# A one-core float32 decoder block: more Strassen steps, x laid out by channel, the inverse root applied after the products

## The chip, the cores and the metric

The kernel runs on one core of a Trainium2 chip. The metric is the device time of one execution in microseconds (us), the median over runs. The profile of one execution is read beside it. The engines are PE (TensorE; its weight loads are listed as PEld and overlap the products), DVE (VectorE), ACT (ScalarE), POOL (GpSimd) and SP (SyncE, which here only issues DMAs). Each engine takes its own instructions strictly in order; they wait for each other by semaphores.

## The reference

For 256 tokens of 4096 channels, all in float32:

```python
h = rmsnorm(x, norm_w)                                   # x * 1/root(mean x^2 + eps) * norm_w
proj = einsum('bsd,de->bse', h, w_in)                    # 4096 -> 20480
u_p, z_p, u_c, b_c, c_c, z_c, g_logit = split(proj)      # 6 parts of 2048, one of 8192
y_pool = causal_multiscale_pool(u_p, pool_w, pool_scale) * silu(z_p)
y_conv = causal_gated_shortconv(u_c, b_c, c_c, conv_w, conv_b) * silu(z_c)
br = einsum('bsnc,ncd->bsnd', stack(y_pool, y_conv), w_branch)   # 2 x (2048 -> 4096)
merged = sum(sigmoid(g_logit + gate_b) * br)
x = x + einsum('bsd,de->bse', merged, w_out)             # 4096 -> 4096
return rmsnorm(x, final_norm_w)
```

The pooling takes a trailing mean of 2, 4, 8 or 16 tokens less the token itself, and then a 512x512 map for each of four groups. The short convolution is B * conv3(C * u).

## The kernel before

**Units and steps.** The output of every large product is cut into units of 1024 columns: 20 for w_in (named cu, cc, cb, cz for the convolution, pz, pu for the pool, g for the gates), 8 for w_branch (b0_c, b1_c), 4 for w_out (o0 to o3). A unit runs over its inner dimension in steps of 256 rows: 16 steps, or 8 in a branch unit. Each step loads one block of weights of 256x1024 (1 MB) on SP's queue into one of three buffers of `raw` (`NRAW = 3`, loads in turn, so a block takes the place of the one three steps earlier as soon as that one is prepared).

**High and low parts.** PE multiplies in fp32r, a rounded form. So every float32 operand is split: ACT writes the rounded high part, `act(h, q)` (line 62), and DVE the remainder, `sub(l, q, h)` (line 65). Each product is three matmuls: high by high, high by low, low by high. The parts of the weights lie in `ring`, a ring of 60 pieces of 256 columns; the parts of x (later of y and of the merged rows) stay in `arena`.

**P and S steps.** A P step is the plain product: two k blocks, two token blocks, two column halves, 24 matmuls of 128x512. Its preparation is one rounding on ACT and one subtraction on DVE, each 128x2048, and takes 16 pieces of the ring. An S step is one level of Strassen (Winograd's form): seven products, 21 matmuls. Its preparation is more work on DVE: the three blocks that are used as they are get one 128x1536 subtraction, four sums of weight blocks are made (one add of 128x1024 and two of 128x512), and the sums are rounded on ACT and subtracted on DVE two at a time (128x1024 each). It takes 12 + 8 + 8 pieces. Where two products of x operands are needed in sums, these are made once per operand (`sums_s`).

**Where the products go.** PSUM has four banks `sums` for results that need no recombination (called E) and four banks `shared` for the S products that are used in several places (called F). At the end of a unit ACT evacuates E with the inverse root of the norm as a scale, and `combine` (line 388) takes F apart: one copy on ACT, four operations of 128x512 and one of 128x2048 on DVE. `shared` also serves for transposes (line 416), the pooling (580 to 583, 601) and the start. After `combine` the unit's epilogue (`epi`) is put into a queue, of which one item is issued after every six matmuls (`TICK = 6`): gates, sigmoid, taps of the convolution, transposes, stores.

**Order.** All instructions are issued in the order in which the Python code makes them. `pump` (1003) lets preparation run up to three steps ahead of the matmuls (`AHEAD = 3`), as far as `raw` and `ring` have room. `Ring.alloc` (174) hands out and frees blocks in order. In a w_in unit of before the sequence is PPPPP SPSPSPSPSPS: 10 P and 6 S; the first unit has no S, but six N steps (plain products over both sets of banks). Branch units are PPPPPSPS. Altogether 154 S steps in 448.

**Start.** x arrives by tokens on SP's queue, and 64 transposes on PE (900) turn it; the S operands of x are prepared during the first unit, after the root is known (`x_stage`, `x_sums`, `x_fill`); PE also spreads the root over partitions (888).

Of the kernel before, what the change touches and what calls it, by code (L numbers as in the profile page):

```python
# [25 lines left out]
NP_X, NS_X = 10, 6  # L43
NP_Y, NS_Y = 6, 2
RING = 60
NRAW = 3
AHEAD = 3
# [3 lines left out]


@with_exitstack
def hybrid_block(ctx: ExitStack, tc: tile.TileContext, x, norm_w, w_in, pool_w, pool_scale,
                 conv_w, conv_b, gate_b, w_branch, w_out, final_norm_w, out):
    nc = tc.nc
    xf, of = x[0], out[0]
    win, wbr, wout, pw = w_in[0], w_branch[0], w_out[0], pool_w[0]
# [23 lines left out]
    def move(dst, src):  # L82

        return pin(nc.gpsimd.dma_start(dst, src))

# [9 lines left out]
    arena = sb("arena", [P, (4 * NP_X + 7 * NS_X) * KB], F32R)  # L95
# [5 lines left out]
    V = sb("V", [P, 2, NH])  # L101
    sa = sb("sa", [P, 8, P])
    ident = sb("ident", [P, P])
    par_n = sb("par_n", [P, 32])
    par = sb("par", [P, 64])
    rin = sb("rin", [P, 2])
    rout = sb("rout", [P, 2])
    ssq = sb("ssq", [P, 2, 8])
    ossq = sb("ossq", [P, 2, 5])


    PE0 = psum.tile([P, 2, NH], F32, name="sums0")
    PE1 = [psum.tile([P, NH], F32, name=f"sums1{n}") for n in range(2)]
# [3 lines left out]

# [5 lines left out]

    xhome = (R, E, Y, R)

    def xs(a, b, t=None):
        q = xhome[a // NU]
        s = slice(a % NU, (b - 1) % NU + 1)  # L130
        return q[:, :, s] if t is None else q[:, t, s]

    def load_x(a, b, queue=None):
        pin((queue or nc.sync).dma_start(xs(a, b), xrows[:, :, a:b]))
# [7 lines left out]


    def p_slot(i):

        return arena[:, 4 * KB * i:4 * KB * (i + 1)].rearrange("p (a k t c) -> p a k t c", a=2, k=2, t=2)

    def s_slot(i):

        o = 4 * KB * NP_X + 7 * KB * i  # L150
        return arena[:, o:o + 7 * KB].rearrange("p (a o c) -> p a o c", a=2, o=7)

    def sp_slot(i):

        o = 4 * KB * NP_X + 7 * KB * i
        return arena[:, o:o + 4 * KB].rearrange("p (a k t c) -> p a k t c", a=2, k=2, t=2)

    Q3, Q5, Q6, Q7, A12, A22, A11, A21 = range(8)

    class Operand:  # L160


        def __init__(self, kind, view, region):
            self.kind, self.view, self.region = kind, view, region
            self.ready = False

    busy = {}


    class Ring:  # L170
# [3 lines left out]
        def alloc(self, n):  # L174
            at = self.head if self.head + n <= self.size else 0
            for a, m, _ in self.live:
                if at < a + m and a < at + n:
                    return None
            if at == 0 and self.head + n > self.size and any(a >= self.head for a, _, _ in self.live):
                return None  # L180
            block = [at, n, False]
            self.live.append(block)
            self.head = at + n
            return block

        def release(self, block):
            block[2] = True
            while self.live and self.live[0][2]:
                self.live.pop(0)
# [3 lines left out]
    def piece(block, off, n):  # L193
        o = (block[0] + off) * KB
        return ring[:, o:o + n * KB]


    class Step:
        def __init__(self, unit, kind, src=None, op=None, **kw):
            self.unit, self.kind, self.src, self.op = unit, kind, src, op  # L200
            self.__dict__.update(kw)
            self.raw = None
            self.pre = []

        def micros(self):

            r = None if self.src is None else self.raw

            def both(block):
                self.h = piece(block, 0, 8).rearrange("p (k n) -> p k n", k=2)  # L210
                self.l = piece(block, 8, 8).rearrange("p (k n) -> p k n", k=2)
                self.block = block
                q = r.rearrange("p (k n) -> p k n", k=2)
                if self is steps[0]:
                    for k in range(2):
                        act(self.h[:, k], q[:, k])
                        sub(self.l[:, k], q[:, k], self.h[:, k].bitcast(F32))
                else:
                    act(self.h, q)
                    sub(self.l, q, self.h.bitcast(F32))  # L220

            if self.kind in "PN":
                return self.pre + [(16, None, both)]
            if self.kind == "S":
                q = r.rearrange("p (i n) -> p i n", i=4)
                tv = V

                def sums(_):
                    add(tv, q[:, 0:1].to_broadcast([P, 2, NH]), q[:, 1:3])

                def direct(block):
                    self.bd = block
                    self.dh = piece(block, 0, 6).rearrange("p (i n) -> p i n", i=3)
                    self.dl = piece(block, 6, 6).rearrange("p (i n) -> p i n", i=3)
                    act(self.dh, q[:, 1:4])
                    add(q[:, 0], tv[:, 0], q[:, 2])
                    sub(self.dl, q[:, 1:4], self.dh.bitcast(F32))
                    add(q[:, 1], q[:, 0], q[:, 3])

                def t13(block):  # L240
                    self.b13 = block
                    self.h13 = piece(block, 0, 4).rearrange("p (i n) -> p i n", i=2)
                    self.l13 = piece(block, 4, 4).rearrange("p (i n) -> p i n", i=2)
                    act(self.h13, tv)
                    sub(self.l13, tv, self.h13.bitcast(F32))

                def t24(block):
                    self.b24 = block
                    self.h24 = piece(block, 0, 4).rearrange("p (i n) -> p i n", i=2)
                    self.l24 = piece(block, 4, 4).rearrange("p (i n) -> p i n", i=2)  # L250
                    act(self.h24, q[:, 0:2])
                    sub(self.l24, q[:, 0:2], self.h24.bitcast(F32))

                return self.pre + [(0, None, sums), (12, None, direct), (8, None, t13), (8, None, t24)]
            if self.kind == "B":
# [7 lines left out]
                return [(16, lambda: self.unit.flags.get("base"), parts)]  # L263
            if self.kind == "M":
                g = self.g
                e = E.rearrange("p a n -> p (a n)")[:, g * 1024:(g + 1) * 1024].rearrange(
                    "p (k t) -> p k t", k=4)

                def weights(block):
                    self.bw = block  # L270
                    self.h = piece(block, 0, 8).rearrange("p (k n) -> p k n", k=4)
                    self.l = piece(block, 8, 8).rearrange("p (k n) -> p k n", k=4)
                    q = r.rearrange("p (k n) -> p k n", k=4)
                    act(self.h, q)
                    sub(self.l, q, self.h.bitcast(F32))

                def pooled(block):
                    self.ba = block
                    self.ah = piece(block, 0, 4).rearrange("p (k t) -> p k t", k=4)
                    self.al = piece(block, 4, 4).rearrange("p (k t) -> p k t", k=4)  # L280
                    act(self.ah, e)
                    sub(self.al, e, self.ah.bitcast(F32))

                return [(16, None, weights), (8, lambda: self.unit.flags.get(f"pooled{g}"), pooled)]

        def groups(self):

            gs = []
            if self is steps[0]:

                for k in range(2):
                    for i in range(3):
                        for t in range(2):
                            for n in range(2):
                                cs = slice(n * NH, (n + 1) * NH)
                                ah, al = self.op.standing(k, t)
                                h, l = self.h[:, k, cs], self.l[:, k, cs]
                                gs.append([("E", t, n), [((ah, h), (al, h), (ah, l))[i]], None])
                gs[-1][2] = [self.block]
            elif self.kind in "PN":  # L300
                for t in self.toks:
                    for n in self.halves:
                        cs = slice(n * NH, (n + 1) * NH)
                        mm = {"E": [], "F": []}
                        for k in range(2):
                            ah, al = self.op.standing(k, t)
                            h, l = self.h[:, k, cs], self.l[:, k, cs]
                            mm["F" if self.kind == "N" and k == 0 else "E"] += [(ah, h), (ah, l), (al, h)]
                        gs += [[(b, t, n), mm[b], None] for b in "FE" if mm[b]]
# [881 lines left out]
    while queue:  # L1191
        f = queue.popleft()
        if f:
            f()
# [61 lines left out]
```

## Time and profile before

| | |
|---|---|
| median of three runs | 2446.13 us (2446.05 to 2447.01) |
| span of the profiled execution, first to last instruction | 2444.0 us |
| granted clock, mean over the span | 0.997 |
| HBM read, written | 508.61 MB, 23.07 MB |
| wait of ACT `ring` for PE `sums` | 333.9 us in 137 waits |
| wait of DVE `ring` for ACT `ring` | 260.3 us in 251 waits |
| wait of PE `sums` for DVE `ring` | 11.7 us in 12 waits |

The profiled execution's time is its span; what the runs have above it, 2.1 us at the median, lies before the first and after the last instruction. In the rows of groups the columns are line, engine, operation, output<-input with shapes, count; then busy us and mean ns of one; then the idle time of the engine just before, with what ended most of it. In the rows of stretches each engine has its busy us and in brackets its instructions.

### The profile page before, as it was taken

The page shows a single profiled execution, that of the slowest core. Times are in us where ns is not written, and L with a number is a line of the kernel's source. Part 1 is how long each engine was busy: PE and PEld are TensorE (multiplying, and loading weights), DVE is VectorE, ACT ScalarE, POOL GpSimd, SP SyncE. Part 2 cuts the span into 40 slices and gives each one's busy share as a digit, 9 for nine tenths or more (in the row PEclk, how much of TensorE's full clock was granted, in tenths as well). Part 3 has the DMA queues.
Part 4 walks back from the last instruction along what each step waited for, and adds up shares of the span by engine and source line. Part 5 has one row for each costly group of instructions (what it writes and reads, how often), then busy time and mean ns, then how long its engine had stood idle before and what let it go on. Part 6 is the DMA issues. An engine that isn't in the chain of part 4 may idle for free.

```text
span 2444.0 us, 27058 instructions
## 1 busy us (share of the span) xinstructions
PE 2406.5 (98%) x10722; PEld 1987.0 (81%) x10722; DVE 2041.9 (84%) x1713; ACT 1296.7 (53%) x1089; POOL 61.6 (3%) x129
## 2 busy tenths in 40 slices
PE   9999999999999999999999999999999999999997
PEld 7888788888788888888888888887788888878886
DVE  5889789789888878968888888888888778888897
ACT  6545455555455545455555545555564455555554
POOL 0100000000000000000000000000000000000000
PEclk9999999999999999999999999999999999999999
DMA  7455565555566555556666666566667666666666
GB/s 276 172 207 204 180 219 207 206 207 189 189 214 216 193 194 212 193 189 224 236 224 219 220 229 232 195 240 229 239 231 252 219 233 238 227 229 225 232 229 260
DMA packets 137536, 533.45 MB, mean 218 GB/s; under 512 B 8832, under 2 KB 9408, under 8 KB 134592
## 3 DMA queue, kind: packets, MB, share of 16 engines
q1 hardware_dynamic: 126640, 483.42, 55.6%
q0 software_dynamic: 10432, 47.22, 5.2%
q8 instruction: 84, 1.38, 0.2%
q10 hardware_dynamic: 336, 1.07, 0.1%
q14 instruction: 44, 0.36, 0.0%
HBM read 508.61 MB, written 23.07 MB: 218 GB/s over the span
## 4 chain that ended last, share of the span: by engine, by line
PE 85%; DVE 6%; ACT 3%; issue 3%; DMA 2%; SPq 0%; POOL 0%; DVEq 0%; ACTq 0%; POOLq 0%
PE sums L1052 68%; PE shared L1052 15%; DVE ring L65 2%; ACT ring L62 2%; DVE R L65 2%; DMA raw<-in_w_out_dram 1%; PE shared L416 1%; PE shared L601 1%; DVE V L65 1%; DMA Y<-in_x_dram 1%; DVE raw L65 1%; ACT E L62 0%; DMA raw<-in_w_branch_dram 0%; PE shared L900 0%; ACT arena L62 0%
## 5 line engine op out<-in xcount | busy, mean ns | idle before, releaser
L1052 PE MATMUL sums<-ring,arena 128*128 128x512 f32 x8370 | 1968.0, 390 | 14.9 <-DVE ring L65 11.7
L1052 PEld LDWEIGHTS sums<-ring,arena 128*128 128x128 f32 x8370 | 1569.0, 188 | 345.2 <-DVE ring L65 16.4
L65 DVE TENSOR_TENSOR ring<-raw,ring 128x2048 fp32r<-128x2048 f32 (+2 forms) x607 | 1139.9, 1881 | 322.2 <-ACT ring L62 251.5
L62 ACT ACTIVATE ring<-raw 128x2048 fp32r<-128x2048 f32 (+2 forms) x607 | 946.8, 1585 | 756.6 <-PE sums L1052 306.1
L1052 PE MATMUL shared<-ring,arena 128*128 128x512 f32 x1884 | 475.1, 389 | 1.7 <-DVE ring L65 1.7
L1052 PEld LDWEIGHTS shared<-ring,arena 128*128 128x128 f32 x1884 | 353.4, 188 | 76.4 <-DVE ring L65 2.7
L62 ACT ACTIVATE ring<-V 128x1024 fp32r<-128x1024 f32 (+1 forms) x157 | 163.8, 1043 | 187.6 <-DVE V L65 164.1
L65 DVE TENSOR_TENSOR ring<-V,ring 128x1024 fp32r<-128x1024 f32 (+1 forms) x157 | 188.6, 1202 | 2.4 <-PE sums L1052 1.5
L65 DVE TENSOR_TENSOR V<-raw 128x1024 f32<-128x1024 f32 x154 | 187.8, 1219 | 0.9 <-DMA raw<-in_w_in_dram 0.9
L65 DVE TENSOR_TENSOR raw<-raw 128x512 f32<-128x512 f32 x154 | 106.6, 692 | 5.3
L65 DVE TENSOR_TENSOR raw<-V,raw 128x512 f32<-128x512 f32 x154 | 106.5, 692 | 4.8
L65 DVE TENSOR_TENSOR R<-R,E 128x2048 f32<-128x2048 f32 x41 | 93.9, 2291 | 8.6 <-DMA E<-in_x_dram 3.4
L65 DVE TENSOR_TENSOR R<-R,shared 128x512 f32<-128x512 f32 x90 | 61.7, 685 | 2.1
L62 ACT ACTIVATE E<-sums,rin 128x512 f32<-128x512 f32 (+1 forms) x60 | 45.3, 822 | 1.7 <-PE sums L1052 1.7
L62 ACT ACTIVATE arena<-sa 128x512 fp32r<-128x512 f32 (+1 forms) x24 | 17.3, 721 | 53.0 <-DVE sa L65 44.6
L65 DVE TENSOR_TENSOR R<-R,Y 128x2048 f32<-128x2048 f32 x17 | 38.9, 2289 | 0.3
L62 ACT ACTIVATE R<-R 128x2048 f32<-128x2048 f32 x8 | 15.4, 1919 | 42.6 <-DVE R L65 42.6
L416 PE MATMUL shared<-ident,R 128*128 128x128 f32 x192 | 28.3, 278 | 5.7 <-DVE R L65 5.7
L416 PEld LDWEIGHTS shared<-ident,R 128*128 128x128 f32 x192 | 23.7, 143 | 11.8 <-issue 4.5
L65 DVE TENSOR_TENSOR arena<-sa,arena 128x512 fp32r<-128x512 f32 (+1 forms) x24 | 19.3, 805 | 8.2 <-ACT arena L62 8.2
L601 PE MATMUL shared<-ring 128*128 128x512 f32 x96 | 22.1, 389 | 0.0
L62 ACT ACTIVATE E<-R 128x1024 f32<-128x1024 f32 (+1 forms) x10 | 13.9, 1396 | 15.1 <-DVE R L65 15.1
(151 smaller groups left out, 429.3 us busy)
## 6 DMA issues: line engine op xcount, KB each, us to landing
raw<-in_w_in_dram SPq DMA_DIRECT2D x319, 1024.0 KB, 4.8
raw<-in_w_branch_dram SPq DMA_DIRECT2D x64, 1024.0 KB, 5.6
raw<-in_w_out_dram SPq DMA_DIRECT2D x64, 1024.0 KB, 5.3
gates_d<-R POOLq DMA_DIRECT2D x8, 1024.0 KB, 8.9
raw<-in_pool_w_dram SPq DMA_DIRECT2D x4, 1024.0 KB, 5.2
Y<-in_gate_b_dram POOLq DMA_DIRECT2D x8, 512.0 KB, 11.3
Y<-gates_d POOLq DMA_DIRECT2D x4, 1024.0 KB, 10.3
E<-gates_d POOLq DMA_DIRECT2D x4, 1024.0 KB, 5.2
```

The source lines that it names most:

```text
L62: return pin(nc.scalar.activation(dst, src, func, **kw))
L65: return pin(nc.vector.tensor_tensor(out=dst, in0=a, in1=b, op=op))
L416: pin(nc.tensor.transpose(shared(j)[:, i * T + t * P:i * T + (t + 1) * P], src[:, t, c:c + P], ident))
L601: pin(nc.tensor.matmul(o, a[:, k, ts], b[:, k], start=(k, i) == (0, 0), stop=(k, i) == (3, 2)))
L1052: pin(nc.tensor.matmul(ps, lhs, rhs, start=n == 0, stop=n == u.total[b] - 1))
```

## The change

The lines below are from the kernel after; "..." marks what is left out.

Units have a text that gives their kinds of steps, and there are 195 S steps:

```diff
-NP_X, NS_X = 10, 6
-NP_Y, NS_Y = 6, 2
+ND, NS, NB = 8, 6, 2
-AHEAD = 3
+AHEAD = 4
+SIX5 = "PPPPPSPSPSPSPSPS"
+SIX4 = "PPPPSPSPSPSPSPSP"
+SEVEN3 = "PPPSPSPSPSPSPSPS"
+EIGHT = "PSPSPSPSPSPSPSPS"
+HOST = "PPPBPPMMPPSPSSPSSPS"
+OUT3 = "PSPSPSPSPSPSSPPP"
+B0 = "PPPPPSPS"
+B1 = "PSPPSPSP"
```

(B and M are the pooling steps.) In order: cz0 SIX5, cb0 EIGHT, cu0 SEVEN3, cc0 EIGHT, cz1 SIX4, cb1 EIGHT, cu1 SEVEN3, cc1 EIGHT, pz0 SIX4, pu0 EIGHT, pz1 HOST, pu1 EIGHT, g0_0 HOST, six gate units EIGHT, g1_3 SIX4, the branches B0 and B1 in turn, o0 SIX5, o1 and o2 EIGHT, o3 OUT3.

A step's preparation is cut in two, and ACT's first rounding of step i+1 is issued before the rest of step i. The ring keeps its 60 pieces; blocks are freed part by part:

```diff
+    def first(self):          # P: act(h, q) 128x2048;  S: act(dh, q[:, 0:3])
+    def rest(self):
+        if self.kind == "P":
+            def lows(_):
+                for ks in self.ks:
+                    sub(self.l[:, :, ks], self.q[:, :, ks], self.h[:, :, ks].bitcast(F32))
+        if self.kind == "S":
+            def direct(_):
+                sub(self.dl, self.q[:, 0:3], self.dh.bitcast(F32))
+            def t13(block):
...
+                add(q[:, 1::2], q[:, 3:4].to_broadcast([P, 2, NH]), q[:, 1:3])
+                act(self.h13, q[:, 1::2])
+                add(q[:, 2], q[:, 1], q[:, 2])
+            def t24(block):
...
+                add(q[:, 0], q[:, 2], q[:, 0])
+                act(self.h24, q[:, 0::2])
+                sub(self.l13, q[:, 1::2], self.h13.bitcast(F32))
+                sub(self.l24, q[:, 0::2], self.h24.bitcast(F32))
...
+    lay(0, steps[0].pre + steps[0].first())
+    for i in range(len(steps)):
+        if i + 1 < len(steps):
+            lay(i + 1, steps[i + 1].first())
+        lay(i, steps[i].rest() + [(None, None, lambda _, i=i: done(i))])
+        if i + 1 < len(steps):
+            lay(i + 1, steps[i + 1].pre)
```

The products of an S step run in the order M2, N3, M1, N7, N5, N4, N6 (the last of a unit: M2, N3, N4, M1, N7, N5, N6); M2, N3 and M1 use the direct part, N7 and N5 the pair `t13`, N4 and N6 the pair `t24`.

The operands of x carry norm_w but no root, which comes in at the joins:

```diff
+    def evacuate(u, t, n):
+        dst = E if u.s else u.dst
+        kw = dict(scale=rin[:, t:t + 1]) if u.scaled else {}
+        act(dst[:, t, n * NH:(n + 1) * NH], PE_[t][n], **kw)
+    def corners(d):
...
+        act(q(0, 1), shared(0))
+        add(q(1, 0), q(0, 1), shared(3))
+        add(q(1, 1), q(1, 0), shared(2))
+        sub(d[:, :, 0:NH], shared(1).rearrange("p (o n) -> p o n", o=1).to_broadcast([P, 2, NH]),
+            d[:, 1].rearrange("p (n c) -> p n c", n=2))
+    def combine(u):
...
+            if u.scaled:
+                for t in range(2):
+                    stt(d[:, t], d[:, t], rin[:, t:t + 1], E[:, t], ALU.mult, ALU.add)
+            else:
+                add(d, d, E)
```

x comes a second time, turned on the host (`xc`), 256 KB for each step of the first unit on SP's queue; the rows by tokens come on POOL's queue and serve only for the squares. The first unit has S steps; 64 + 2 transposes and the spreading of the root go:

```diff
+    def x_operand(j):
+        i = first_order[j]
+        o, q = x_ops[i], xt[:, j % 4]
+        if o.kind == "P":
...
+        else:
+            for k in range(2):
+                act(sa[:, 6 - 2 * k:8 - 2 * k], q[:, 2 - 2 * k:4 - 2 * k], scale=norm_col(2 * i + k))
+            sums_s(sa)
+            parts_of(o, sa[:, 0:o.n])
+    before(2, fetch_rows, 0)
+    before(2, fetch_rows, 1)
+    before(6, square, 0)
...
+    before(13, square, 3)
+    before(13, lambda: rstd_of(ssq, rin, "rin"))
```

Weights are laid out on the host so that a step's block is 8 KB in a row for each partition. silu is one activation of 128x2048 on ACT in place of a sigmoid and a multiplication; the convolution's units run in the order z, B, u, C, and its gates are multiplied by tokens, so that 32 transposes fall away; pool_scale is a column scale of an ACT copy:

```diff
+    def silu_y():
+        return gap(1) + [lambda: act(Y, Y, AF.Silu)]
+        def b_epi(u):
...
+            return gap(1) + [lambda: mul(R, R, Y)] + gap(4) + transposes(R, copy) + [lambda: move(g_d[c], Y)]
+        def c_epi(u):
+            items = gap(1) + [lambda: mul(R, R, Y)] + gap(3) + [lambda: move(E, g_d[c])]
...
+            return items + gap(4) + [lambda: mul(Y, Y, E), lambda: put(y_d[1, c], chan(Y))]
```

Epilogues of the gate, branch and out units are as before.

More of the change, by code (lines that the diff above doesn't have):

```diff
@@ L780, in hybrid_block @@
         branch_unit(1, c)
-    last_y = units[-2], units[-1]
     for c in range(4):
@@ L961, in hybrid_block @@
[L961 to L982 removed]
+        q = rows_tile(c)
@@ L987, in hybrid_block, with lay, done @@
         s.load_index = i
-    state = dict(limit=0, nl=0, np=0, micros=None, prepared=0, now=0, mm=0)
+    state = dict(limit=1, nl=0, mm=0, now=0)
+    work = deque()
+    def lay(i, items):
+        work.extend((i, size, guard, fn) for size, guard, fn in items)
+    def done(i):
+        steps[i].prepared = True
+    lay(0, steps[0].pre + steps[0].first())
[5 more added lines that the diff above has]
+            lay(i + 1, steps[i + 1].pre)
     queue = deque()
@@ L1035, in pump, with flush @@
                 return
-    for s in steps:
-        s.prepared = False
+    def flush():
+        while queue:
+            f = queue.popleft()
+            if f:
+                f()
     def tick():
@@ L1053, in multiply @@
             u.seen[b] = n + 1
-        for block in release or ():
-            rg.release(block)
+        for part in release:
+            rg.release(part)
         state["mm"] += len(mm)
     def after_group(u, b):
-        if b[0] == "E" and u is not last:
-            t = b[1]
-            if u.closed(("E", t, 0), ("E", t, 1)) and not u.flags.get(f"e{t}"):
-                u.flags[f"e{t}"] = True
-                evacuate(u, t)
+        if u is not last:
+            if b in u.total and u.closed([b]) and b not in u.flags:
+                u.flags[b] = True
+                if b[0] == "E":
+                    evacuate(u, b[1], b[2])
+                elif u.closed(FB):
+                    flush()
+                    corners(u.dst)
         while state["mm"] >= TICK:
```

856 lines of the change are left out of this document (318 added, 538 removed).

## The prediction

> **What bounds the kernel now.** I read the page first, then busy time by stretches, the chain of waits, groups by form, and the timeline of one join between two gate units.
>
> ```profile
> span 2444.0 us, 27058 instructions
> PE 2406.5 (98%) x10722; PEld 1987.0 (81%) x10722; DVE 2041.9 (84%) x1713; ACT 1296.7 (53%) x1089; POOL 61.6 (3%) x129
> ```
>
> ```profile
> 0.00:15.00 15.00, 10.50 (x33) 7.45 (x34) 5.87 (x8) 7.07 (x9) 2.01 (x9) 1.00 0.85 314
> 15.00:50.00 35.00, 34.10 (x174) 28.27 (x173) 26.57 (x45) 26.69 (x49) 0.76 (x1) 1.00 0.76 288
> 1394.00:1477.00 83.00, 83.00 (x368) 68.73 (x367) 68.30 (x52) 43.64 (x33) 1.06 (x2) 1.00 0.62 220
> 1700.00:1780.00 80.00, 72.81 (x312) 57.71 (x311) 70.28 (x68) 44.71 (x39) 5.90 (x11) 1.00 0.68 236
> 2432.00:2444.00 12.00, 0.00 (x0) 0.00 (x0) 5.19 (x13) 2.80 (x6) 0.00 (x0) 0.61 0.80 320
> ```
>
> PE sets the time. A gate unit (1394 to 1477) has PE busy throughout and DVE for 68.3 of 83.0; PE idles at the start, 7.2 us at the first branch units, and 12 us behind its last matmul.
>
> ```profile
> 1403.71 27.20 PE sums L1052 x120
> ```
>
> A large matmul costs 27.20/120 = 0.2267 us: a P step 5.44, an S step 4.76, a pair 10.20.
>
> **What goes from PE.**
>
> ```profile
> L1052 PE MATMUL sums<-ring,arena 128*128 128x512 f32 x8370 | 1968.0, 390 | 14.9 <-DVE ring L65 11.7 <-ACT ring L62 2.4 <-ACT E L62 0.8
> L1052 PE MATMUL shared<-ring,arena 128*128 128x512 f32 x1884 | 475.1, 389 | 1.7 <-DVE ring L65 1.7
> L900 PE MATMUL shared<-ident,R 128*128 128x128 f32 x32 | 5.5, 313 | 1.4 <-DMA R<-in_x_dram 1.4
> L416 PE MATMUL shared<-ident,R 128*128 128x128 f32 x192 | 28.3, 278 | 5.7 <-DVE R L65 5.7
> ```
>
> With 36 + 96 more, large matmuls were 448 x 24 - 154 x 3 + 96 = 10386. Now 195 x 3 are saved: 10263, 123 fewer, 27.9 us. Of transposes go 64 (line 900; this row has half) and 32 (line 416), at 28.3/192 = 0.15 us by busy time, overlaps in; I take 0.1, together 9.6, and 0.9 for six small ones. PE has 38.4 us less.
>
> **What DVE gets.** Timeline of DVE, then groups:
>
> ```profile
> 1407.15 1.40 DVE L65 TENSOR_TENSOR R<-R,shared 128x512 f32<-128x512 f32 x2
> 1409.91 2.29 DVE L65 TENSOR_TENSOR R<-R,E 128x2048 f32<-128x2048 f32 x1
> 1412.24 2.29 DVE L65 TENSOR_TENSOR R<-R,Y 128x2048 f32<-128x2048 f32 x1
> 1414.44 2.28 DVE L65 TENSOR_TENSOR ring<-raw,ring 128x2048 fp32r<-128x2048 f32 x1
> 1420.86 1.22 DVE L65 TENSOR_TENSOR V<-raw 128x1024 f32<-128x1024 f32 x1
> 1426.34 1.23 DVE L65 TENSOR_TENSOR ring<-raw,ring 128x1024 fp32r<-128x1024 f32 x1
> 1431.03 1.23 DVE L65 TENSOR_TENSOR V<-raw 128x1024 f32<-128x1024 f32 x1 [0.60 <-DMA raw<-in_w_in_dram]
> ```
>
> ```profile
> L65 DVE TENSOR_TENSOR ring<-raw,ring 128x1536 fp32r<-128x1536 f32 x154 | 269.9, 1753 | 13.0 <-ACT ring L62 12.7
> L62 ACT ACTIVATE ring<-raw 128x2048 fp32r<-128x2048 f32 x297 | 566.9, 1911 | 215.8 <-PE sums L1052 134.4 <-issue 39.8 <-DVE R L65 13.3
> L62 ACT ACTIVATE ring<-raw 128x1536 fp32r<-128x1536 f32 x154 | 228.9, 1487 | 243.4 <-PE sums L1052 146.4 <-issue 75.4 <-DMA raw<-in_w_in_dram 10.8
> L62 ACT ACTIVATE ring<-V 128x1024 fp32r<-128x1024 f32 x154 | 162.9, 1058 | 187.6 <-DVE V L65 164.1 <-PE sums L1052 18.0 <-PE shared L1052 4.7
> L65 DVE TENSOR_TENSOR raw<-raw 128x512 f32<-128x512 f32 x154 | 106.6, 692 | 5.3
> L77 DVE SCALAR_TENSOR_TENSOR sa<-R 128x512 f32<-128x512 f32 x4 | 2.7, 682 | 0.0
> ```
>
> One S step is 6.7 us of DVE (1420.86 to 1426.34 + 1.23), a P 2.2 (1412.24 to 1414.44); within S: direct part 1.75, adds 1.25, 0.65, 0.65, subtractions 1.15, 1.2. A P-S pair is 8.9 against PE's 10.20, and 41 more S add 41 x 4.5 = 185 us. At the join DVE has corners (0.65 + 0.65 and one subtraction of 2x512 out of PSUM, not in the trace: from 0.7, one 512, to 1.4, two; I take 1.2) = 2.5, and two scaled joins of 128x1024 (from 1.15, the plain one, to 1.36, twice 682 ns; I take 1.15) = 2.3; a gate unit adds its bias, 2.2. An EIGHT gate unit is then 8 x 8.9 + 7.0 = 78 of PE's 81.6: it fits in sum, and the question is the lead. silu on ACT (1.9 like any 128x2048, plus a table load) is covered: ACT is 53% busy.
>
> **The lead.** In the new order the direct rounding of the next S waits until PE has freed the second product (1.36 us into an S). Rounding 1.49, then 6.7 of DVE: the last subtraction is out at 9.55. PE wants it at 10.20 + 15 x 0.2267 + 0.23 = 13.83. The ring allows DVE 4.3 us of lead, no more. A second ring closes over the loads:
>
> ```profile
> raw<-in_w_in_dram SPq DMA_DIRECT2D x319, 1024.0 KB, 4.8
> raw<-in_w_out_dram SPq DMA_DIRECT2D x64, 1024.0 KB, 5.3
> ```
>
> The end of an S frees the buffer for the P three steps on: 4.8 landing, 1.9 that P's rounding on ACT, behind it the next S's rounding 1.06, subtractions 1.15 + 1.2: 10.1, against 10.20. So lost lead returns at 0.1 us a pair. I take 2.5 at a join (bounds 0 and 4.3). The trace agrees that loads are close: DVE waits for one in the 1431.03 row. The Trainium skill (DMA: Bandwidth & Descriptors, "Anatomy of one DMA") gives an estimate of 2.0 us + bytes/436e9, 4.4 us for this load; by it the loop would be 9.7, lead would be back to 4.3 at most joins, and the total some 25 us lower. The trace has 4.8.
>
> **Joins, t = 0 at a unit's end.** PE runs P to 5.44, S to 10.20, then P. The second matmul of a product takes the low part, so PE wants the S's first pair of subtractions at 7.71, the second at 9.07, the next P's subtraction ("lows") at 10.43. Before, five P follow a join, each with 5.44 - 2.2 = 3.2 us of DVE to spare: that is the work's cover in the gate row above (83.00 of 83.00). Now an S follows at once, and the order in which the built program issues its instructions has the join on DVE ahead of the S's rest, in two ways. DVE ends the lows of the new unit's first P at -1.5 with the lead taken.
>
> (a) Direct part and two adds first, done at 2.2: corners 4.7, rest of S 7.7, joins 10.0, bias 12.2, lows 14.4: 4.0 late; without bias 1.8.
> (b) Corners first, which wait for the last matmul, with the S's direct part queued behind them: 2.6, direct and adds 6.25, joins 8.55, first subtraction 10.35 (2.6 late), 11.55, bias 13.75, lows 15.95 (2.9 more): 5.5. Joins behind the whole S: 5.6. Without bias 3.3 or 3.4.
>
> Counting places in the order: gate units 3 x 4.0 + 5.5 + 2 x 5.6 = 28.7; cc0, cb1, cc1, pu0 1.8 + 3 x 3.3 = 11.7. Into b1 (four times) corners, E add, rest, the product with Y, lows: 3.9 each, 15.6. Out units add two 2.2 us operations later: 3.7, 5.2, 3.7. cu0 begins with P, but joins and a product stand before its second P's lows: 9.3 for 5.67, 3.6; cz1 and pz0 have 16 taps each:
>
> ```profile
> L77 DVE SCALAR_TENSOR_TENSOR Y<-shared,par,Y 128x254 f32<-128x254 f32 x16 | 7.7, 482 | 0.6
> ```
>
> 4 each after their lead; 12 with cu0 and cu1. The bands:
>
> ```profile
> 114.54 0.27 DVE L561 TENSOR_REDUCE cnt<-sa 128x1 f32<-128x128 f32 x1
> 119.52 4.49 DVE L65 TENSOR_TENSOR ring<-raw,ring 128x2048 fp32r<-128x2048 f32 x2
> ```
>
> They hold DVE for 5.0 us, waiting for POOL; five P hid that. They now precede a P's lows in cb0 and pu1: 9.3 (no lead there) + 8.4 = 17.7. Joins: 28.7 + 11.7 + 15.6 + 12.6 + 12 + 17.7 = 98.
>
> **The opening.**
>
> ```profile
> 8.29 1.06 ACT L62 ACTIVATE ring<-raw 128x1024 fp32r<-128x1024 f32 x1 [1.56 <-DMA raw<-in_w_in_dram]
> 106.53 2.66 PE L1052 MATMUL sums<-ring,arena 128*128 128x512 f32 x11
> L77 DVE SCALAR_TENSOR_TENSOR arena<-shared,par_n,arena 128x256 fp32r<-128x256 f32 x20 | 8.7, 478 | 9.6 <-ACT arena L62 9.6
> L65 DVE TENSOR_TENSOR sa<-sa 128x128 f32<-128x128 f32 x28 | 6.9, 287 | 0.3
> L62 ACT ACTIVATE arena<-sa 128x896 fp32r<-128x896 f32 x7 | 6.7, 954 | 27.6 <-DVE sa L65 27.5
> L65 DVE TENSOR_TENSOR arena<-sa,arena 128x896 fp32r<-128x896 f32 x7 | 7.6, 1091 | 4.1 <-ACT arena L62 4.1
> ```
>
> Before, unit 1 ends at 106.9, 20 behind 384 x 0.2267. Now its S steps come at once, and eight S operands of x cost DVE four sums, a wait for ACT and a subtraction, about 2.8 each. SP's queue carries 256 KB of x with each 1 MB of weights, 1.31 MB at the 314 GB/s of the first stretch, 4.2 us a step; POOL's two loads of rows wait for nothing and meet the first of them. With five P steps ahead, from the first S on (about 30 us) DVE has 6 x 6.7 + 5 x 2.2 + 8 x 2.8 + 11 for other operands, squares and root = 84, so the unit ends near 117: 34 behind 366 x 0.2267 = 83 (bounds 16, if DVE's waits overlap, and 42).
>
> **The sum.** Before: 10386 x 0.2267 = 2354 + 27 for bands and transposes + 12.7 end + 20 opening, which leaves 30 of stalls; I keep 25 (branch fills, pooling, o0). After: 2326.3 + 7 + 16 + 12.7 + 34 + 98 + 25 = 2519 for the span. The runs stand 2.1 above it: **2521 us**, own range 2460 (half the joins, 24 opening) to 2570.
>
> **Rivals.** *The cover holds* (faster, 0.21): the ring frees its pieces sooner than I read it, so that at a join DVE is over 6.5 us ahead (2.5 + the 4.0 of a join with bias; from there on no join stalls), and it makes that lead up again in the unit from its 3.6 us of slack and the P at the start of every other kind of unit: 2444.0 - 38.4 + 2.1 = 2408, and up to 2440 if a third of the joins still stall. For it: DVE fits in every unit's sum. Against: 4.3 by the ring, and lows queued behind joins. *The loads bind* (0.1): at w_out's 5.3 the load loop is 10.6, 0.4 over PE in some 165 pairs: 2521 + 66 = 2587. For it: higher landing in that half. Against: blocks now lie in a row. *No lead is gained from rounding ahead* is the forecast itself: the subtraction, not the rounding, is late, so that part does not do what its words say. The convolution's new fetch of 1 MB on POOL's queue (twice) is issued twelve items of six matmuls, 16 us, ahead of its use, its store more than a unit ahead; against a landing of about 5 us as in the two rows above it is costed at nothing, and at 5 each if that cover were gone. *PE cools*:
>
> ```profile
> 2113.58 1.89 PE L416 MATMUL shared<-ident,R 128*128 128x128 f32 x8 [2.00 <-DVE R L65]
> 2115.12 2.55 PE L1052 MATMUL sums<-ring,arena 128*128 128x512 f32 x6
> ```
>
> After that wait six matmuls took 0.425 each. With a dozen joins of over 3.4 us, 3.4 us at half speed each would add 20: 2541, in my range. The Trainium skill (TensorE: Matmul & The Clock Gate, "Part 1: The HAM clock gate") says an idle window of about 3.4 us halves the clock and a busy one releases it; the trace agrees in kind, at a shorter wait.
>
> **Chances.** Forecast with cooling 0.67, loads 0.1, cover holds 0.21, no change 0.02. Measurement tells 0.2% (5 us) from none: faster 0.21, same 0.03, slower 0.76. Range 2405 to 2590.
>
> **What would show it.** PE waits for DVE `ring` rise from 11.7 us to over 80, at joins and for lows; gate units of 85 to 88 us; unit 1 ends at 110 to 120; DVE near 88%; 4-us gaps right after P-S of a new unit. Gate units of 82 us would prove the lead argument wrong; an opening under 100, that term.

## The result, and the profile after

The kernel after takes **2653.01 us** (median of four runs, 2649.02 to 2656.09) against 2446.09 for the kernel before beside it: a ratio of **1.0846, 95% interval 1.083 to 1.0861**. The forecast was 2521 with a range up to 2590: the direction was right, the size far too small (75 us forecast, 207 measured).

Head of the page of the kernel after:

```profile
span 2654.4 us, 26478 instructions
PE 2454.0 (92%) x10497; PEld 1981.1 (75%) x10497; DVE 2206.3 (83%) x1871; ACT 1365.0 (51%) x1200; POOL 61.1 (2%) x131
```

PE, busy for 98% before, is busy for 92%. No other engine has taken its place: DVE is at 83%, where it was at 84%. So PE waits, and a share of busy time doesn't say for whom. Stretches of the kernel after (the first unit, one gate unit, the end; columns as before):

```profile
7.20:122.10 114.90, 96.76 (x367) 74.52 (x368) 93.15 (x117) 69.83 (x82) 4.92 (x21) 0.93 0.60 230
1315.90:1409.10 93.20, 85.14 (x362) 68.35 (x361) 79.19 (x63) 46.19 (x37) 1.07 (x2) 0.96 0.53 197
2640.00:2654.00 14.00, 1.34 (x6) 0.76 (x5) 7.24 (x16) 3.55 (x7) 0.00 (x0) 0.62 0.76 300
```

A gate unit takes 93.2 us where it took 83.0, with DVE busy for 79.2 of them (78 were forecast), and its granted clock is 0.96: PE was also slowed, not only idle. Groups by form:

```profile
L843 PE MATMUL sums<-ring,arena 128*128 128x512 f32 x7827 | 1910.5, 398 | 114.1 <-DVE ring L55 101.5 <-ACT E L52 6.2 <-ACT ring L52 4.1
L843 PE MATMUL shared<-ring,arena 128*128 128x512 f32 x2340 | 620.6, 400 | 67.9 <-DVE ring L55 59.5 <-ACT ring L52 5.3 <-ACT R L52 1.8
L52 ACT ACTIVATE ring<-raw 128x2048 fp32r<-128x2048 f32 x256 | 490.7, 1917 | 776.0 <-DMA raw<-in_w_in_dram 492.4 <-DMA raw<-in_w_out_dram 104.7 <-PE sums L843 78.3
L55 DVE TENSOR_TENSOR ring<-raw,ring 128x1024 fp32r<-128x1024 f32 x392 | 469.1, 1222 | 203.2 <-ACT ring L52 197.4 <-PE sums L843 2.5
```

PE waits 161 us for DVE (`ring`), where it waited 13. The wait in the third row has no counterpart before: ahead of its roundings of P steps ACT is idle for 776 us, of which some 600 for the step's load. The fourth shows who pays: DVE's subtractions of the S's sums wait 197 us for ACT, which stands behind that load.

To see where PE loses its time I took the distance from each large matmul to PE's next instruction and counted what it has above 0.2267 us (distances over 0.26; those of 0.415 to 0.45, a matmul at half speed, apart). "Joins" are a unit's steps up to the one behind its first S, "inside" is the rest.

| us | opening, idle | joins, idle | inside, idle | half speed, all |
|---|---|---|---|---|
| after | 23.9 | 147.5 | 59.5 | 48.6 |

The same count gives 33 us idle and 2 at half speed for the whole kernel before. One join in the timeline of the kernel after, where gate unit g0_1 begins at 1315.85:

```profile
1316.10 1.41 DVE L55 TENSOR_TENSOR R<-R,shared 128x512 f32<-128x512 f32 x2 [1.53 <-ACT R L52]
1317.55 1.22 DVE L55 TENSOR_TENSOR R<-shared,R 128x1024 f32<-128x1024 f32 x1
...
1318.69 1.75 DVE L55 TENSOR_TENSOR ring<-raw,ring 128x1536 fp32r<-128x1536 f32 x1
1320.47 2.68 DVE L55 TENSOR_TENSOR raw<-raw 128x1024 f32<-128x1024 f32 x3
...
1323.07 2.43 DVE L55 TENSOR_TENSOR ring<-raw,ring 128x1024 fp32r<-128x1024 f32 x2
...
1325.42 2.48 DVE L67 SCALAR_TENSOR_TENSOR R<-R,rin,E 128x1024 f32<-128x1024 f32 x2
...
1327.01 0.39 PE L843 MATMUL sums<-ring,arena 128*128 128x512 f32 x1
1327.93 2.29 DVE L55 TENSOR_TENSOR R<-R,Y 128x2048 f32<-128x2048 f32 x1
1330.14 3.95 DVE L55 TENSOR_TENSOR ring<-raw,ring 128x2048 fp32r<-128x2048 f32 x2
...
1332.48 7.90 PE L843 MATMUL sums<-ring,arena 128*128 128x512 f32 x26 [5.08 <-DVE ring L55]
```

This is the forecast's variant (b) in its order, with the joins behind the whole S: corners, the S's rest, joins, bias, and only then the lows that PE has wanted since 1327. PE goes on 16.6 us after the unit's start; 15.95 was forecast. The last row has the part that I left out of the sum: 26 matmuls in 7.90 us are 0.30 each, since some of them ran at half speed after the wait.

### The profile page after: what moved, and what is told of

Same layout as the page of the kernel before. It is cut to its first block, busy times and chain, and to the rows that moved or that the text cites. A ratio compares the mean times of both kernels' runs of the same rounds, so it can differ in the third digit from the quotient of the medians.

```text
span 2654.4 us, 26478 instructions
## 1 busy us (share of the span) xinstructions
PE 2454.0 (92%) x10497; PEld 1981.1 (75%) x10497; DVE 2206.3 (83%) x1871; ACT 1365.0 (51%) x1200; POOL 61.1 (2%) x131
## 5 line engine op out<-in xcount | busy, mean ns | idle before, releaser
L843 PE MATMUL sums<-ring,arena 128*128 128x512 f32 x7827 | 1910.5, 398 | 114.1 <-DVE ring L55 101.5
L843 PEld LDWEIGHTS sums<-ring,arena 128*128 128x128 f32 x7827 | 1491.4, 192 | 461.4 <-DVE ring L55 132.1
L52 ACT ACTIVATE ring<-raw 128x1024 fp32r<-128x1024 f32 (+2 forms) x843 | 1158.8, 1413 | 1126.5 <-DMA raw<-in_w_in_dram 525.7
L55 DVE TENSOR_TENSOR ring<-raw,ring 128x1024 fp32r<-128x1024 f32 (+2 forms) x843 | 1369.0, 1668 | 239.9 <-ACT ring L52 233.8
L843 PE MATMUL shared<-ring,arena 128*128 128x512 f32 x2340 | 620.6, 400 | 67.9 <-DVE ring L55 59.5
L843 PEld LDWEIGHTS shared<-ring,arena 128*128 128x128 f32 x2340 | 444.9, 192 | 182.4 <-DVE ring L55 76.6
L55 DVE TENSOR_TENSOR raw<-raw 128x512 f32<-128x512 f32 (+1 forms) x585 | 508.7, 870 | 19.2
L55 DVE TENSOR_TENSOR R<-R,shared 128x512 f32<-128x512 f32 x52 | 35.7, 687 | 62.4 <-ACT R L52 43.2
L52 ACT ACTIVATE E<-sums,rin 128x512 f32<-128x512 f32 x80 | 50.8, 682 | 7.6 <-PE sums L843 7.5
L55 DVE TENSOR_TENSOR arena<-sa,arena 128x512 fp32r<-128x512 f32 (+2 forms) x28 | 24.4, 872 | 27.5 <-ACT arena L52 27.5
L55 DVE TENSOR_TENSOR R<-R,E 128x2048 f32<-128x2048 f32 x19 | 43.5, 2287 | 0.2
L67 DVE SCALAR_TENSOR_TENSOR R<-R,rin,E 128x1024 f32<-128x1024 f32 x28 | 34.7, 1279 | 0.0
L529 PEld LDWEIGHTS shared<-ring 128*128 128x128 f32 x96 | 17.7, 188 | 7.8 <-DVE ring L55 2.8
L52 ACT ACTIVATE R<-R 128x2048 f32<-128x2048 f32 (+1 forms) x10 | 17.3, 1734 | 9.7 <-DVE R L55 9.6
```

Of the source, the lines that this page charges most:

```text
L52: return pin(nc.scalar.activation(dst, src, func, **kw))
L55: return pin(nc.vector.tensor_tensor(out=dst, in0=a, in1=b, op=op))
L67: return pin(nc.vector.scalar_tensor_tensor(out=dst, in0=a, scalar=s, in1=b, op0=op0, op1=op1, **kw))
L529: pin(nc.tensor.matmul(o, a[:, k, ts], b[:, k], start=(k, i) == (0, 0), stop=(k, i) == (3, 2)))
L843: pin(nc.tensor.matmul(ps, lhs, rhs, start=n == 0, stop=n == u.total[b] - 1))
```

## The experiments

All times are medians of two runs, each beside the kernel before on the same chip (2445.1 to 2445.8). The diffs are against the kernel after unless another is named.

| us | time | opening, idle | joins, idle | inside, idle | half speed, all |
|---|---|---|---|---|---|
| e1 six after five | 2534.9 | 24.0 | 45.3 | 47.3 | 23.4 |
| e2 in order | 2595.0 | 27.5 | 82.0 | 70.7 | 36.8 |
| e3 joins later | 2596.2 | 25.0 | 87.1 | 77.0 | 27.0 |
| e5 P ahead only | 2646.8 | 25.4 | 114.3 | 86.0 | 43.8 |
| e6 S ahead only | 2599.3 | 28.6 | 101.2 | 48.7 | 45.8 |
| e7 ring of 52 | 2693.4 | 26.9 | 146.3 | 94.2 | 48.6 |
| e9 ring of 52, four buffers | 2616.4 | 26.3 | 137.8 | 35.8 | 41.6 |
| e10 = e2 + e3 + e4 | 2552.3 | 27.0 | 65.0 | 57.2 | 29.8 |
| e11 = e1 + e2 | 2508.9 | 26.8 | 29.3 | 41.5 | 16.0 |
| e13 = e11, six S operands | 2483.5 | 22.4 | 28.2 | 20.9 | 13.6 |

**Six S steps behind five P** (e1).

```diff
+SIX4 = SEVEN3 = EIGHT = SIX5          # PPPPPSPSPSPSPSPS
+OUT3 = "PPPSPSPSPSPSSPPP"
+B1 = "PPPSPSPS"
```

> Every unit of sixteen steps begins with at least three and nearly always five P steps and has six S steps, as before (164 S steps in all, the branch units b1 begin PPP); everything else of the change stays. Queue theory (PE waits at joins because corners, joins and bias stand on DVE ahead of the first S and the next lows): the join stalls of 147 us and most of the 48 us of half-speed matmuls go; 93 more matmuls cost 21 us; 2654 - 147 + 25 - 35 + 21, about 2470 to 2520. Load theory (the circle of raw buffers, at 10.1 to 10.6 against 10.20, holds every P-S pair): pairs still come in runs of five, stalls inside the units stay or grow, above 2560. Total theory (DVE has too much work with 195 S): 31 S less takes 140 us of DVE, about 2500 too, but then PE's stalls inside the units fall and not those at the joins.

2534.85 us, ratio 1.0363 (1.0333 to 1.0393). The joins went from 147.5 to 45.3 and the half-speed time to 23.4, as by the queue theory, but 15 us short of its range: the time inside the units fell by only 12. Gate units behind a gate unit took 83.0 to 84.3 us; the rest sat in the first unit and around the branches.

**Rounding in order** (e2).

```diff
-    lay(0, steps[0].pre + steps[0].first())
     for i in range(len(steps)):
-        if i + 1 < len(steps):
-            lay(i + 1, steps[i + 1].first())
-        lay(i, steps[i].rest() + [(None, None, lambda _, i=i: done(i))])
-        if i + 1 < len(steps):
-            lay(i + 1, steps[i + 1].pre)
+        lay(i, steps[i].pre + steps[i].first() + steps[i].rest() + [(None, None, lambda _, i=i: done(i))])
```

> The rounding of step i+1 is issued after the rest of step i, as before; sequences and all else as in the kernel after. My forecast said that rounding ahead gains no lead. If it does no harm either: within 15 us of 2653. If it does harm (the S's rest stands in the code's queue behind the 16 pieces that the next P's rounding needs, so DVE cannot take it before the corners): joins become 2 to 4 us shorter in 12 units, 2600 to 2630. If it does what its words say (a subtraction never waits for its rounding), taking it away makes DVE wait 1.5 to 1.9 us for ACT in each step: over 2700.

2595.02 us, ratio 1.0609 (1.0578 to 1.064): 58 us come back for the order alone. DVE at the join into gate unit g1_1, which begins at 1398.05 in this kernel:

```profile
1399.98 2.56 DVE L55 TENSOR_TENSOR ring<-raw,ring 128x1024 fp32r<-128x1024 f32 x2
1402.46 1.40 DVE L55 TENSOR_TENSOR R<-R,shared 128x512 f32<-128x512 f32 x2
...
1405.16 2.48 DVE L67 SCALAR_TENSOR_TENSOR R<-R,rin,E 128x1024 f32<-128x1024 f32 x2
1407.55 2.29 DVE L55 TENSOR_TENSOR ring<-raw,ring 128x2048 fp32r<-128x2048 f32 x1
```

The first S's last two subtractions stand ahead of the corners now; in the kernel after they began 4.3 us behind the corners' end. DVE waits for ACT's roundings 17 us more than in the kernel after (256.1 against 239.1), so the gain that the words "one step ahead" suggest is small beside the harm.

**Joins in pieces, one pair apart** (e3), in all units but cb, cc, pu and b1, whose epilogues must end before the next S.

```diff
-        combine(u)
-        queue.extend(u.epi(u))
+        for t, n in ((0, 5), (1, 7)):
+            queue.extend(gap(n) + [lambda t=t, d=d: stt(d[:, t], d[:, t], rin[:, t:t + 1], E[:, t],
+                                                         ALU.mult, ALU.add)])
...
+        queue.extend(gap(5) + u.epi(u))      # the gates' bias in two halves, 7 items apart
```

> The two joins after cz, cu, pz, gate, b0 and out units, and the gates' bias, are cut into pieces of one token block each and issued one P-S pair apart behind the new unit's first steps; corners stay where they are. Queue theory: the stalls at these joins fall from 4 to 8 us to 1 to 2 (only corners are ahead of the S), half-speed matmuls fall below 25 us; 2540 to 2580. Total or load theory: the pieces take the same DVE time out of pairs without slack, the stalls move into the units, over 2630.

2596.18 us, ratio 1.0614 (1.0583 to 1.0644). At the join into g0_1 (1299.24):

```profile
1311.01 1.28 DVE L67 SCALAR_TENSOR_TENSOR R<-R,rin,E 128x1024 f32<-128x1024 f32 x1
1311.15 6.87 PE L843 MATMUL sums<-ring,arena 128*128 128x512 f32 x29 [0.41 <-DVE ring L55]
...
1322.89 1.28 DVE L67 SCALAR_TENSOR_TENSOR R<-R,rin,E 128x1024 f32<-128x1024 f32 x1
```

PE's wait of 5.08 us has become 0.41, with the join's pieces 12 us apart. Over the kernel the joins lost 60 us of idle time, but the pairs inside gave 17 back: queue theory by kind, less than it asked in size, since a pair has little slack to pay from.

**The bands elsewhere** (e4): made at the start of pz0 and g0_0.

> The bands are made at the start of pz0 and of g0_0, units that begin with three or four P, in place of the starts of cb0 and pu1. My forecast priced them at 9.3 and 8.4 us in those two joins. Queue theory: cb0 and pu1 lose about 5 us each of stall and 1 us each of half-speed time, and pz0 and g0_0 gain under 3 in all: 2642 to 2648. Rival, that the bands were covered anyway: 2653.

2650.65 us, ratio 1.0836 (1.0805 to 1.0868), within the spread of the kernel after's runs. The losses at the joins of cb0 and pu1 fell by 6.3 and 5.8 us with half speed counted, as expected, but 2.5 us came back inside cb0, and pz0 became 5 us longer: the four P at its start did not cover the bands, the wait mostly moved.

**Which rounding harms** (e5, e6).

```diff
+        early = i + 1 < len(steps) and steps[i + 1].kind == "P"     # "S" in e6
+        if early:
+            lay(i + 1, steps[i + 1].first())
         lay(i, steps[i].rest() + [(None, None, lambda _, i=i: done(i))])
         if i + 1 < len(steps):
+            if not early:
+                lay(i + 1, steps[i + 1].first())
             lay(i + 1, steps[i + 1].pre)
```

> Only the rounding of a P step is issued before the rest of the step ahead of it; an S's direct rounding comes in its own turn. Taking all of rounding ahead away gave 58 us back. Placement theory: the harm is that an S's rest stands behind the next P's rounding, in the code's queue (it needs 16 free pieces) and on ACT (it needs the P's load): then this kernel keeps the whole harm, 2640 to 2670. If the harm is with the S's early rounding: 2590 to 2605.

> The counterpart: only an S's direct rounding is issued before the rest of the P ahead of it, the P's rounding in its own turn. Placement theory: nothing of an S stands behind a P's load or 16 pieces any more, 2585 to 2605, as without rounding ahead. If the S's early rounding is what harms: 2640 to 2670.

2646.75 us (1.0823, 1.0791 to 1.0854) with the P's ahead, 2599.29 (1.0628, 1.0598 to 1.0659) with the S's. The waits of ACT for weights, in us, times and longest, of e5 and then of e6:

```profile
ACT ring L52 <- DMA raw<-in_w_in_dram: 548.0, 133, 10.5
```

```profile
ACT ring L52 <- DMA raw<-in_w_in_dram: 31.9, 18, 4.8
```

It is the P's rounding. Ahead of an S's rest, it stands on ACT in front of the S's two roundings of sums, and waits there for its load.

**The ring and the buffers** (e7, e8, e9). e7 is the control for the other two: four buffers fit only beside a smaller ring.

```diff
-RING = 60
-NRAW = 3
+RING = 52
+NRAW = 4                      # e8, e9
-        if i + 1 < 16:        # e9: x comes with its own step's weights
-            fetch_x(i + 1)
+        if 0 < i < 16:
+            fetch_x(i)
```

> The kernel after with 52 pieces in the ring in place of 60: control for the next run, and a test of how far the ring sets the lead. If the ring's pieces set DVE's lead at a join: 8 pieces fewer, a third of a P-S pair, at least 2 us more in each of some 20 joins and stalls in each pair: over 2700. If the circle of loads sets the lead: within 15 us of 2653.

> Four buffers of raw with the ring of 52. Load theory: a P's load is issued a step earlier (at the end of the P four steps back), ACT no longer waits for it with the S's sums queued behind, and the kernel comes out 40 to 80 us below the ring of 52 with three buffers. Ring theory (the 16 free pieces come last): within 15 us of it, though ACT's waits for loads (526 us in the kernel after) fall below 150 us.

> Four buffers and a ring of 52 again, with the block of x fetched together with the weights of its own step, so that none of its four slots is overwritten before it is used (in the run before, the first unit lost 74 us to that, and x was wrong). Behind the first unit that run took 2493.7 us against 2568.2 with three buffers. Load theory: the first unit is back at 112 to 120 us and the gain shows in the whole: 2610 to 2635. Rival (the 74 us behind the first unit were won because its delay let the loads run ahead once): the gain shrinks below 20 us, over 2670.

e7: 2693.41 us (1.1013, 1.0981 to 1.1045); e8: 2692.54 (1.101, 1.0978 to 1.1042); e9: 2616.37 (1.0698, 1.0667 to 1.0729). e8 looked like a clear no to the load theory and wasn't one: loading four steps ahead, it fetched x over a block that was still to be used, so that it computed with the wrong x, and the first unit took 189 us in place of 118 (117 in e9, where x comes in time). Behind the first unit it was 74 us faster than its control; e9, with x in time, is **77 us** faster in the whole. Rounding of the P steps in e7, then in e9:

```profile
L52 ACT ACTIVATE ring<-raw 128x2048 fp32r<-128x2048 f32 x256 | 491.0, 1918 | 767.6 <-DMA raw<-in_w_in_dram 422.0 <-DMA raw<-in_w_out_dram 115.0 <-PE sums L843 103.6
```

```profile
L52 ACT ACTIVATE ring<-raw 128x2048 fp32r<-128x2048 f32 x256 | 489.6, 1913 | 246.3 <-PE sums L843 185.8 <-PE shared L843 22.0 <-PE shared L529 11.4
```

The load is gone from the list, and the idle time inside the units fell from 94.2 to 35.8; that of the joins hardly moved (146.3 to 137.8). Behind the first unit e7 and e9 have the same instructions in the same order on PE, ACT and DVE, so the loads alone make the difference there. It is a difference at 52 pieces of ring; for 60 no run gives it. So there are two causes in two places: the loads, nearly all inside the units, and the order of the work at the joins. Eight pieces of ring fewer cost 40 us, between what the two theories asked; 35 of it is idle time inside the units.

**Both mended** (e10), and **the rest of the change** (e11, e12).

> The kernel after, 195 S steps, with rounding in order, the joins in pieces one pair apart, and the bands at the start of pz0 and g0_0: the three edits gave 58, 57 and 2 us alone. Queue theory with two separate causes (loads held by rounding ahead; joins ahead of the S on DVE): they add, 2535 to 2560. If both edits take away the same stalls: 2575 to 2595.

> Six S steps a unit behind up to five P, and rounding in order: what is left of the change is the opening, the joins with the root, silu, the host layout and ring parts. 10356 matmuls are 2348 us, transposes and bands 23, start and end 21, the opening 33; if the joins and the fills cost no more than the 28 us of before: 2453. If the remaining edits have a price of their own (bands behind two P, S operands of y and the merged rows filled among six S): 2465 to 2490.

> The same with the joins in pieces and the bands at the start of pz0 and g0_0. With up to five P behind each join there is little left to gain at joins: 0 to 10 us below the run before it; above it if pieces spread over pairs without slack cost more than five P hide.

e10: 2552.25 us (1.0436, 1.0406 to 1.0466): the three edits took away 101 us, where they had taken 117 one by one, so the two causes nearly add. Its gate units g1_1 to g0_3 lose 1.1 us each at the join and nothing inside, 82.7 us where the kernel before took 83.0: such a unit can be fed with eight S steps. e11: 2508.9 (1.0259, 1.0229 to 1.0289), 19 us above the worse of its two expectations. e12: 2518.2 (1.0297, 1.0267 to 1.0327); the joins went from 29.3 to 17.3 us, but the time inside the units from 41.5 to 57.1: pieces on pairs without slack cost more than five P would have hidden.

**What is left in e11** (e13 to e15).

```diff
-ND, NS, NB = 8, 6, 2
+ND, NS, NB = 10, 6, 0          # e13: six S operands of sixteen; branches B0 only
...
-            parts_of(o, sa[:, 0:o.n])                    # e14: the remainder of an x operand
+            act(o.view[:, 0], sa[:, 0:o.n])              # behind its step's own preparation
...
+            sub(o.view[:, 1], sa[:, 0:o.n], o.view[:, 0].bitcast(F32))
```

> As the run with six S steps and rounding in order (2508.9), with six S operands among the sixteen of x and of the merged rows in place of eight, and two of eight in each branch, as before (160 S steps, 12 matmuls or 2.7 us more). If the fills of S operands (sums, a wait for ACT, a remainder, about 3.4 us of DVE each) hold the units g1_3, b1_3 and o0 and the opening: 15 to 30 us less, 2480 to 2495. If they are hidden: 2507 to 2514.

> As the run before, and in the first unit DVE's remainder of an x operand comes after its step's own preparation (DVE waits 14 us there for ACT), and the bands are made in pieces spread over unit cc0 and over pu1. DVE theory of the opening (84 us of work behind 30 us): the first unit ends 8 to 14 us earlier, cb0 loses its 7 us of stall: 15 to 22 us below the run before. If the opening is bound by its loads: under 10 us.

> All 195 S steps and eight S operands, rounding in order, joins in pieces, and the two edits of the run before. Against 2552 without the last two: the same 12 to 20 us less, 2530 to 2540. Against the run before: if S steps at every second place are worth their DVE work once the queues are in order, this one is as fast or faster; if not, it stays 30 us or more above.

e13: 2483.53 us (1.0157, 1.0128 to 1.0187), 25 less than e11: 21 inside the units g1_3, b1_3, o0 and o3, where the operands of y and of the merged rows are filled, and 5 in the opening. e14: 2484.49 (1.0161, 1.0132 to 1.0191) and e15: 2560.08 (1.047, 1.044 to 1.0501), both a miss: putting the remainder later made the first unit 6 us longer in e14 and 15 in e15, not 8 to 14 shorter, and with the bands gone from it cb0 still lost 6.4 us in e14, of 7.8 (in e15, behind the longer first unit, 0.4). Why the first unit grew stays open. e15 also stays 76 us above e14, where 30 or more were to mean that S steps at every second place aren't worth their work on DVE. None of the versions beats the kernel before; e13 is still 38 us above it, and no run takes apart what the root at the joins, silu, the host's layout and the convolution's new order have in that.

## Why the prediction was right in direction and wrong in size

**PE's work and DVE's sums: right.** 10263 large matmuls, DVE at 2206 us of work, a gate unit at 79 of DVE; 78 was forecast. Of the signs that the prediction named, PE's waits for DVE came (161 us), but gate units took 90 to 94 us in place of 85 to 88.

**The step that failed: the load of a P step, rounded one step ahead, was priced at nothing.** The prediction worked out "10.1, against 10.20. So lost lead returns at 0.1 us a pair", and then carried on with 2.5 us of lead at a join and no loss inside the units. The sum of the circle was right. In the stretch from 1425 to 1465 of the kernel after, ACT and DVE show it, and the load's landing there:

```profile
1441.26 5.19 ACT L52 ACTIVATE ring<-raw 128x2048 fp32r<-128x2048 f32 x4 [5.14 <-DMA raw<-in_w_in_dram]
1451.41 3.82 ACT L52 ACTIVATE ring<-raw 128x2048 fp32r<-128x2048 f32 x3 [4.95 <-DMA raw<-in_w_in_dram]
```

```profile
1444.16 6.23 DVE L55 TENSOR_TENSOR ring<-raw,ring 128x1024 fp32r<-128x1024 f32 x4 [3.43 <-ACT ring L52]
```

```profile
DMA to landing us min/median/max: 4.7/6.3/7.2
```

From one P's rounding to the next are 10.15 us. What failed is the 4.8: it is the median of before, where ACT waited little for loads and a late one went into the lead of five P steps. In the kernel after a quarter of the 1 MB loads take over 6 us, before it was a sixth, and a gain of 0.1 us a pair makes up for little. That a late load then costs PE its whole delay is not shown: in this stretch one load took 7.0 us, and PE lost nothing. What shows the price of the loads is e9 over e7, 77 us. The rival *the loads bind* had this mechanism and with 66 us a price near it; its chance of 0.1 was the error, with the reason against it ("blocks now lie in a row") taken from the layout and not from a row of landings. That price is for 52 pieces of ring, and 58 of it is idle time inside the units. In the kernel after all of that idle time is 59.5 us, 13.8 of it not of the loads (see the stalls below), so the loads cost less inside its units; what they cost it in all stays open.

**Rounding ahead is the same step, and it cost 58 us** (e2; 54 by e6). The prediction has "*No lead is gained from rounding ahead* is the forecast itself", at no price. "The subtraction, not the rounding, is late" held, but I looked only for a gain. Ahead, the P's rounding puts its load in front of the S's sums on ACT and, with it, the whole rest of the first S behind the corners on DVE. With the same three buffers and the P's rounding back in its turn, ACT's waits for loads of w_in fall from 525.7 us to 31.9 (e6), and without any rounding ahead the joins lose 82.0 us (e2), less than the 98 of the sum. That the kernel's code lets the S's rest stand behind the 16 pieces of ring which that rounding needs is what the code says; no run separated the pieces from ACT's wait, but the joins of e9, which lose 137.8 us with the waits for loads gone, speak for the order.

**The joins: the right order, 98 forecast, 147.5 measured.** The gate joins stall for 4.7 to 7.7 us where 4.0 to 5.6 were listed (40.3 against 28.7), b1 for 31.1 against 15.6 (13 of it in b1_3, where ACT waits 5.9 us for a load and fills come on top), and units that were not on the list (pz1, g0_0, g1_3, b0_0, o0) for another 12. The lead was nearly the one assumed: at the six gate joins DVE ended the lows of the new unit's first P 1.2 or 1.3 us ahead of the unit's end, 1.5 was taken. What the list lacked is the corners' wait for ACT. It had three gate joins in variant (a) and got three; this is the one into g1_1, which begins at 1409.07:

```profile
1410.67 2.86 ACT L52 ACTIVATE ring<-raw 128x2048 fp32r<-128x2048 f32 x2 [2.73 <-DMA raw<-in_w_in_dram]
1413.44 0.58 ACT L52 ACTIVATE R<-shared 128x512 f32<-128x512 f32 x1
```

```profile
1414.05 1.41 DVE L55 TENSOR_TENSOR R<-R,shared 128x512 f32<-128x512 f32 x2 [2.49 <-ACT R L52]
1415.50 1.23 DVE L55 TENSOR_TENSOR R<-shared,R 128x1024 f32<-128x1024 f32 x1
```

ACT's copy of the first corner stands behind the next P's rounding, which waits for its load, and DVE is done with the corners 7.7 us after the unit's start in place of 4.7. These three joins lost 22.8 us in place of 12.0, nearly the whole excess of the gate joins, and at all four joins into b1 DVE waited 2.5 to 6.3 us in the same way. DVE's waits for copies of this kind are 43.2 us in the kernel after and 3.5 in e6. Bands were 17.7 in the list; cb0 and pu1 together lost 19.4, half of it without any bands (e4).

**Half speed was a rival's 20 us and left out of the sum; it is 48.6.** I expected a dozen waits over 3.4 us. There were 34 stretches of half speed, 243 matmuls at 0.427 us. The Trainium skill (TensorE: Matmul & The Clock Gate, "Part 1: The HAM clock gate") names an idle window of about 3.4 us; here a single gap of 2.2 us (at 1859) was followed by eight matmuls at half speed, so the measurement decides, and shorter waits have to be counted, though not every one of them is followed by half speed (last section).

**Kept stalls: 25 forecast, 59.5 measured.** Besides the loads, two things were missing: the last S of a unit wants its second pair of sums two products earlier, which is 0.8 to 1.8 us late in twelve units (13.8 us), and eight S operands to fill in place of six, 21 us inside the units by e13 beside e11.

**The opening: nearly right.** Unit 1 ends at 122.1, forecast 117, 39 behind its matmuls in place of 34; the difference is half speed (7.6).

From the forecast's span of 2519 these are 49 for joins, 41 for half speed outside the first unit, 35 for stalls inside and 5 for the first unit: 130 of the missing 135.

## What to carry to other kernels

A circle of buffers that closes within 1% of the bottleneck's period can be a second bottleneck rather than cover: price it by the upper quarter of the landings, taken where loads overlap, and not by their median. An instruction issued earlier on an in-order engine brings its own wait with it; before moving it, list what comes to stand behind it on that engine, and on those that follow. An experiment that gives no change is read by stages before it counts: e8's gain of 74 us was hidden behind a loss of the same size in another unit.

## What the runs showed of the hardware

Half speed sets in after shorter waits than I took: most gaps of 2.2 us and more were followed by 5 to 13 matmuls at 0.427 us, but three of 2.3 to 2.8 us (at 58.8, 1873.9 and 2365.7) were not. A stretch lost 1.4 us on average, so by an estimate from that a wait of 3 us costs about half as much again. Of two loads of 1 MB issued 2.2 us apart (from 1446 to 1459 in the kernel after) the first landed after 4.7 to 4.8 us and the second after 5.2 to 6.4; the two before them, with a gate unit's store and the next bias on POOL's queue just ahead, took 7.0 and 7.3.
